# The low halves of the weights' chunks in the rwkv stage: from GpSimd to VectorE

## The chip, the cores and the metric

The kernel runs on one core of a Trainium2 chip. The metric is the time on the device in microseconds (us), the median of three runs. A core has five engines that run side by side, each through a queue of its own in a fixed order: TensorE (PE in the profile; PEld are its weight loads), VectorE (DVE), ScalarE (ACT), GpSimd (POOL) and SyncE (SP), which here only issues DMAs. An engine that waits for a semaphore holds up everything behind it in its queue.

## The reference

Two blocks of a network, one behind the other, over 512 tokens of width 1024, all in 32-bit floats. The first mixes a gated linear recurrence with dilated attention. The second takes its output and a context of 256 tokens, and has three branches: pooling, differential attention and a bidirectional rwkv recurrence, which are gated, summed and projected. A mixture of 32 experts, two per token, ends it. Cut to what matters here:

```
p_l = modulate(x, ...) @ w_in        # 1024 x 7040: pool, q, k, v, rwkv's inputs, three gates
prep_l = rwkv_prepare(rw_l, ...)     # r, k, v, decay, a, b, g from the projections
S = S * w + (S a) b + v k            # per token, 8 heads of 64 x 64, in both directions
mix = sum_n sigmoid(gate_n) * (branch_n @ w_br[n]);  x = x + mod * (mix @ w_out)
x = x + mod * hier_moe(modulate(x, ...))
```

## The kernel before

**Products in two halves.** A weight chunk (128 partitions x 1024 columns, 512 KB) is loaded by `load_chunk` (L293) on SyncE's queue into a raw buffer. `split_chunk` (L300) makes two tiles of it: the high half is a copy by ScalarE into the type float32r (L304), in which TensorE takes it; the low half is raw minus high (L305). `mm3` (L308 to 312) adds three products for each tile: high by high, high by low, low by high. Activations are split the same way by other lines. Each chunk thus has one ScalarE and one subtracting instruction; there are 125 chunks in all that are split (the w_ada and expert weights are not).

**The rwkv stage** begins at L1086. It closes the first block's weight pool and opens one with three buffers each for the high and low halves and two for the raw chunks (L1088); a raw buffer is free again when both halves are made. The recurrence is worked off in 12 batches of two chunks of 64 tokens and one direction (`batch`, L1331). `ph_a` (L1128) loads a chunk's kb and kr, makes the running sum of the decay (cs), its exponentials on ScalarE, the scaled tiles AR and BK, and the masked products AMB. `ph_i` (L1178) sends AMB through DRAM to the layout LT and inverts the triangular matrices by forward substitution on VectorE: 31 steps of a product into Tm (L1194) and a sum into Ti (L1196), each on the result of the last, 372 of each in all. The result goes through DRAM again (ttD) to `ph_b` (L1201), two batches later, which makes the states' products on TensorE and the updates on VectorE.

**Work laid between the batches.** Between and behind the batches stand projections whose chunks are split: rwkv's own inputs for the 512 tokens (`rw_prep`, 14 chunks; `rw_gate`, one), 19 of the 24 chunks of the branch gates (`gate`), the 12 half chunks of q, k and v for the differential attention, and the four of the pooling branch (`feat_tiles`, L1516). That makes 50 chunks from L1086 to L1520. Another 50 are split before, and 25 behind: five gates, 12 of `merge` (L1547), eight of the output projection (L1790). Then come the attention, the merge and the experts, whose weights (192 MB) stream in as they are used.

**What sets the order.** The order of each engine's queue is not that of the program. The Tile planner is called with schedule_with_timeline_sim: it simulates the program by its own costs and gives an engine, whenever it is free there, the next instruction that is ready there. The written order, with the numbers of gates per batch (GB, L1356), sets what is offered first. On the chip each engine then keeps to the planned order and waits where the chip is later than the plan. The DMAs of the batches (kb, kr, LT, ttD, atD) and those of the weights share SyncE's queue, so a weight load that waits for a raw buffer holds up the batch loads behind it.

Of the kernel before, what the change touches and what calls it, by code (L numbers as in the profile page):

```python
# [9 lines left out]
F32 = mybir.dt.float32  # L10
# [3 lines left out]
ALU = mybir.AluOpType  # L14
# [171 lines left out]
def build(tc, A, out, dbg=None, upto=99):  # L186
    with ExitStack() as ctx:
        _build(ctx, tc, A, out, dbg, upto)


def _build(ctx, tc, A, out, dbg, upto):
    nc = tc.nc
    V, SC, GP, PE, SY = nc.vector, nc.scalar, nc.gpsimd, nc.tensor, nc.sync
# [5 lines left out]
    cur = {}  # L199

    def weights(name, bufs, side, raw=None):

        if cur.get("wctx"):
            cur["wctx"].close()
            cur["wctx"] = None
        if bufs:
            cur["wctx"] = ctx.enter_context(ExitStack())
            cur["wp"] = cur["wctx"].enter_context(tc.tile_pool(name=name, bufs=1, side=side, reuse_waits="tile"))
            cur["wb"] = bufs
            cur["wraw"] = raw or bufs  # L210
# [3 lines left out]
    def subpool(name, nb):  # L214

        if cur.get("sub"):
            cur["sub"].close()
            cur["sub"] = None
        if nb is None:
            return  # L220
        cur["sub"] = ctx.enter_context(ExitStack())
        cur["bp"] = cur["sub"].enter_context(tc.tile_pool(name=name, bufs=1, reuse_waits="tile"))
        NB.clear()
        NB.update(nb)

    def scope(name, nb):
        subpool(None, None)
        if cur.get("ctx"):
            cur["ctx"].close()
            cur["ctx"] = None  # L230
        if nb is None:
            return
        cur["ctx"] = ctx.enter_context(ExitStack())
        cur["bp"] = cur["ctx"].enter_context(tc.tile_pool(name=name, bufs=1, reuse_waits="tile"))
        NB.clear()
        NB.update(nb)
# [5 lines left out]
    def psum(name, bufs):  # L242

        if "pctx" in cur:
            cur["pctx"].close()
        cur["pctx"] = ctx.enter_context(ExitStack())
        cur["pp"] = cur["pctx"].enter_context(tc.tile_pool(name=name, bufs=1, space=PSUM, reuse_waits="tile"))
        PB.clear()
        PB.update(bufs)
# [43 lines left out]
    def load_chunk(w, c0, kt=8, name="w", nw=128, k0=0, kn=2):  # L293

        raw = cur["wp"].tile([128, kt, nw], F32, tag="raw", name=name + "r", bufs=cur["wraw"])
        n = c0 // 128 if nw == 128 else c0 // 256 * kn + k0 // 4
        cur["ld"] = SY.dma_start(raw.rearrange("p k n -> p (k n)"), w[n]).ins
        return raw

    def split_chunk(raw, name="w"):  # L300
        kt, nw = raw.shape[1], raw.shape[2]
        hi = cur["wp"].tile([128, kt, nw], F32R, tag="hi", name=name + "h", bufs=cur["wb"])
        lo = cur["wp"].tile([128, kt, nw], F32R, tag="lo", name=name + "l", bufs=cur["wb"])
        SC.activation(hi, raw, AF.Copy)  # L304
        GP.tensor_tensor(lo, raw, hi.bitcast(F32), ALU.subtract)  # L305
        return hi, lo

    def mm3(p, ah, al, bh, bl, start, stop):  # L308
# [42 lines left out]
    def step(n=1):  # L351

        while n and fill:
            try:
                next(fill[0])
                n -= 1
            except StopIteration:
                fill.pop(0)
# [158 lines left out]
    def halves(w, c0):  # L517

        return [split_chunk(load_chunk(w, c0, kt=4, nw=256, k0=4 * kh)) for kh in range(2)]
# [12 lines left out]
    def proj_feat(w, c0, hs, n, dst, nw=256):  # L532

        for b in range(nw // 128):
            hi, lo = split_chunk(load_chunk(w, c0 + 128 * b))
            p = ps("pf")
            for k in range(8):
                mm3(p[:, :n * 128], hi[:, k, :], lo[:, k, :], hs[k][0][:, :n * 128], hs[k][1][:, :n * 128],
                    k == 0, k == 7)
            dst(b, p[:, :n * 128])  # L540
# [545 lines left out]
    weights(None, 0, None)  # L1086
    cp2 = wctx.enter_context(tc.tile_pool(name="c2", bufs=1, side="right", reuse_waits="tile"))
    weights("wp1", 3, "right", 2)  # L1088
    psum("pp2", {"mm": (2, 512), "aux": (3, 512), "ch": (1, 512), "pa": (2, 512)})
    scope("b2a", {})  # L1090
    rp = cur["bp"]
# [269 lines left out]
    def gate(n):  # L1361
        for _ in range(n):
            ngate[0] += 1
            next(gates, None)
# [152 lines left out]

    gate(24 - GL - ngate[0])
    step(99)
    subpool(None, None)  # L1520


# [24 lines left out]
    def merge(n, first=False):  # L1547

        for c in range(4):
            wh, wl_ = split_chunk(load_chunk(A["w_br"], 256 * c, kt=4, nw=256, k0=4 * n, kn=3))  # L1550
            for b in range(2):
                j = 2 * c + b
                pb = ps("pbr")
                th = mt("mth", "mth", 3)
                SY.dma_start(th, thD[:, n, j, :])
                for k in range(4):
                    mm3(pb, wh[:, k, 128 * b:128 * (b + 1)], wl_[:, k, 128 * b:128 * (b + 1)],
                        br[n][k][0], br[n][k][1], k == 0, k == 3)
                if first:
                    V.scalar_tensor_tensor(mg[j], th, 1.0, pb, op0=ALU.add, op1=ALU.mult)  # L1560
                else:
                    V.scalar_tensor_tensor(th, th, 1.0, pb, op0=ALU.add, op1=ALU.mult)
                    V.tensor_tensor(mg[j], mg[j], th, ALU.add)  # L1563
                yield
# [222 lines left out]
    for c in range(4):  # L1787
        po2 = [ps("po2", "aux" if c % 2 else "mm") for _ in range(2)]
        for kh in range(2):
            hi, lo = split_chunk(load_chunk(A["w_out_2"], 256 * c, kt=4, nw=256, k0=4 * kh))  # L1790
# [339 lines left out]
```

## Time and profile before

| | us |
|---|---|
| median of three runs | 1983.2 (1969.7 to 1985.2) |
| the profiled execution, its own time | 1981.6 |
| its span, first to last instruction | 1979.7 |
| TensorE busy (matmuls) | 1755.4, 89% |
| VectorE busy | 1091.5, 55% |
| ScalarE busy | 619.1, 31% |
| GpSimd busy | 526.5, 27% |
| granted TensorE clock, mean | 0.934 of full |

A line of the profile names the source line, the engine, the operation, the tiles it writes and reads (out<-in), their shapes, how often it ran, its busy time and the mean of one in ns, and behind a bar the idle time of its engine ahead of it, with what ended it. Busy shares are means over stages with different limits: what a change in one stage is worth is read in that stage.

### The profile page before, as it was taken

Reading aid. Unit: us, or ns where it says so; the run is one execution under the profiler, and the core shown is the slowest. Engines: PE = TensorE matmul, PEld = TensorE weight load, DVE = VectorE, ACT = ScalarE, POOL = GpSimd, SP = SyncE. Lnnn points to the kernel's source line nnn. Section 1 sums busy time; section 2 is a strip of 40 time slices with the busy share of each in tenths; the row PEclk is TensorE's granted clock in tenths of the full one; section 3 lists DMA queues with packets and bytes.
Section 4 is the critical chain, followed back from the end, with each engine's and each line's share of the span. In section 5 each row is a group of like instructions: output and inputs, shape, how many; then the busy total and the mean of one; then the engine's idle time right before and its main releaser. Section 6 shows DMA issues by size and latency. Waiting matters only on the chain. (4 is left out here: it accounts for less than half of the span.)

```text
span 1979.7 us, 31352 instructions
## 1 busy us (share of the span) xinstructions
PE 1755.4 (89%) x12309; PEld 1246.3 (63%) x12310; DVE 1091.5 (55%) x2364; ACT 619.1 (31%) x1164; POOL 526.5 (27%) x379
## 2 busy tenths in 40 slices
PE   6899998967787887888879998988979999999998
PEld 3874677953565776677667876677954545444544
DVE  4555675275487746777788655776342333332332
ACT  4234454443443222223333233443221111111110
POOL 2510337442335332231331132642310110101010
PEclk8999998988898898889898999999979999999999
DMA  8336513567546445445355338653629999999998
GB/s 298 108 111 218 197 64 103 195 181 250 156 121 171 135 137 122 109 109 137 99 151 152 81 112 280 204 179 111 246 99 387 387 386 386 386 387 386 386 386 289
DMA packets 275295, 415.89 MB, mean 210 GB/s; under 512 B 104876, under 2 KB 126408, under 8 KB 274888
## 3 DMA queue, kind: packets, MB, share of 16 engines
q1 hardware_dynamic: 246248, 383.44, 58.0%
q10 hardware_dynamic: 25568, 16.78, 2.8%
q0 software_dynamic: 3328, 13.63, 2.4%
q8 instruction: 98, 1.61, 0.3%
q14 instruction: 53, 0.43, 0.1%
HBM read 370.26 MB, written 43.53 MB: 209 GB/s over the span
## 5 line engine op out<-in xcount | busy, mean ns | idle before, releaser
L305 POOL TENSOR_TENSOR wl<-wr,wh 128x1024 fp32r<-128x1024 f32 x125 | 308.3, 2473 | 495.8 <-ACT wh L304 455.5
L304 ACT ACTIVATE wh<-wr 128x1024 fp32r<-128x1024 f32 x125 | 131.6, 1054 | 141.2 <-issue 54.9
L1980 POOL TENSOR_TENSOR yl<-ey,yh 128x512 fp32r<-128x512 f32 x30 | 38.4, 1279 | 466.1 <-ACT yh L1979 466.1
L310 PE MATMUL pf<-h2h,wh 128*128 128x512 f32 x344 | 147.8, 430 | 15.6 <-DVE Ti L1196 10.2
L1194 DVE TENSOR_TENSOR Tm<-LT,Ti 128x60 f32<-128x60 f32 (+24 forms) x372 | 116.8, 314 | 76.9 <-DMA LT<-atD 68.2
L311 PE MATMUL pf<-h2l,wh 128*128 128x512 f32 x344 | 144.5, 420 | 0.0
L312 PE MATMUL pf<-h2h,wl 128*128 128x512 f32 x344 | 143.3, 417 | 0.0
L1974 PE MATMUL ped<-wd,hid 128*64 128x512 f32 (+1 forms) x528 | 127.5, 585 | 0.7 <-ACT hid L1958 0.7
L1935 PE MATMUL peg<-wg,hTg 128*64 128x512 f32 x512 | 126.9, 597 | 0.0
L1942 PE MATMUL peu<-wu,hTg 128*64 128x512 f32 x512 | 125.3, 595 | 0.0
L1196 DVE TENSOR_TENSOR Ti<-Ti,Tm 128x60 f32<-128x60 f32 (+24 forms) x372 | 109.3, 294 | 9.1
L2007 DVE TENSOR_TENSOR acc<-acc,pcb 128x512 f32<-128x512 f32 (+1 forms) x124 | 76.0, 665 | 49.1 <-PE pcb L2006 49.0
L310 PEld LDWEIGHTS pf<-h2h,wh 128*128 128x128 f32 x344 | 69.4, 202 | 38.4 <-issue 15.4
L1974 PEld LDWEIGHTS ped<-wd,hid 128*64 128x64 f32 x528 | 39.9, 136 | 70.6 <-issue 65.9
L1942 PEld LDWEIGHTS peu<-wu,hTg 128*64 128x64 f32 x512 | 43.2, 137 | 65.1 <-issue 62.9
L311 PEld LDWEIGHTS pf<-h2l,wh 128*128 128x128 f32 x344 | 68.8, 200 | 18.5 <-issue 3.4
L1935 PEld LDWEIGHTS peg<-wg,hTg 128*64 128x64 f32 x512 | 41.9, 137 | 60.9 <-issue 58.1
L312 PEld LDWEIGHTS pf<-h2h,wl 128*128 128x128 f32 x344 | 68.6, 199 | 18.2 <-issue 2.1
L1282 PE MATMUL pW<-AMB,XV 128*128 128x64 f32 (+1 forms) x256 | 45.2, 335 | 28.7 <-DVE XV L1271 16.9
L1979 ACT ACTIVATE yh<-ey 128x512 fp32r<-128x512 f32 x30 | 18.9, 630 | 163.6 <-DVE ey L1978 90.2
L1915 DVE TENSOR_SCALAR hTg<-pg,gs,sh 128x128 f32<-128x128 f32 x64 | 25.3, 408 | 75.1 <-PE peu L1942 38.4
L1912 ACT ACTIVATE hTg<-pg,sh,gs 128x128 f32<-128x128 f32 x64 | 28.2, 457 | 121.4 <-PE peu L1942 55.4
(961 smaller groups left out, 4475.1 us busy)
## 6 DMA issues: line engine op xcount, KB each, us to landing
wg<-in_w_exp_gate_dram SPq DMA_DIRECT2D x64, 1024.0 KB
wu<-in_w_exp_up_dram SPq DMA_DIRECT2D x64, 1024.0 KB
wd<-in_w_exp_down_dram SPq DMA_DIRECT2D x62, 1024.0 KB
wr<-in_w_in_dram SPq DMA_DIRECT2D x97, 512.0 KB
kb<-kbD SPq DMA_DIRECT2D x24, 384.0 KB
wr<-in_w_out_dram SPq DMA_DIRECT2D x16, 512.0 KB
LT<-atD SPq DMA_DIRECT2D x12, 512.0 KB
thD<-mth ACTq DMA_DIRECT2D x24, 256.0 KB
```

The lines of the kernel that those rows point to most:

```text
L304: SC.activation(hi, raw, AF.Copy)
L305: GP.tensor_tensor(lo, raw, hi.bitcast(F32), ALU.subtract)
L310: PE.matmul(p, ah, bh, start=start, stop=False)
L311: PE.matmul(p, ah, bl, start=False, stop=False)
L312: PE.matmul(p, al, bh, start=False, stop=stop)
L1194: V.tensor_tensor(tmp[:, :nj, :n], bc(LT[:, s, None, ts_], [128, nj, n]), bc(T[:, js, s:s + 1], [128, nj, n]), ALU.mult)
L1196: V.tensor_tensor(T[:, js, ts_], T[:, js, ts_], tmp[:, :nj, :n], ALU.add)
L1282: PE.matmul(pw[e][:, nw * f:nw * (f + 1)], X[:, s, f, :], AMB[:, e, s, f, n0:192], start=True, stop=True)
L1935: mm = PE.matmul(pg[64 * a:64 * a + 64, :], hT[:, k, 64 * a:64 * a + 64], gp[a][k // 4][:, k % 4, :], start=(k == 0), stop=(k == 7), tile_ ...
L1942: PE.matmul(pu[64 * a:64 * a + 64, :], hT[:, k, 64 * a:64 * a + 64], up[a][k // 4][:, k % 4, :], start=(k == 0), stop=(k == 7), tile_posit ...
L1974: PE.matmul(pd[64 * a:64 * a + 64, :], hid[:, m * k + 64 * a:m * k + 64 * a + 64], dn[q][a][:, k, 0:q1 - q0], start=(k == 0), stop=(k == 3 ...
L2007: V.tensor_tensor(acc[i][:, qs], acc[i][:, qs], p, ALU.add)
```

## The change

The engine that makes the low half is looked up in the dictionary `cur` under "lo", and is GpSimd where nothing is set. It is set to VectorE (`V`) when the rwkv stage's pools are opened and taken out again behind the pooling branch. The instruction itself, its operands and its result are the same.

```diff
         SC.activation(hi, raw, AF.Copy)
-        GP.tensor_tensor(lo, raw, hi.bitcast(F32), ALU.subtract)
+        cur.get("lo", GP).tensor_tensor(lo, raw, hi.bitcast(F32), ALU.subtract)
...
     weights("wp1", 3, "right", 2)
+    cur["lo"] = V
     psum("pp2", {"mm": (2, 512), "aux": (3, 512), "ch": (1, 512), "pa": (2, 512)})
...
     gate(24 - GL - ngate[0])
     step(99)
+    cur.pop("lo")
     subpool(None, None)
```

## Rows read from the trace of the kernel before

**Rows 1.** The page: an engine's busy time, and the changed line over the span

```profile
PE 1755.4 (89%) x12309; PEld 1246.3 (63%) x12310; DVE 1091.5 (55%) x2364; ACT 619.1 (31%) x1164; POOL 526.5 (27%) x379
...
L305 POOL TENSOR_TENSOR wl<-wr,wh 128x1024 fp32r<-128x1024 f32 x125 | 308.3, 2473 | 495.8 <-ACT wh L304 455.5
```

**Rows 2.** Busy time by stretch: start:end, length, engines (instructions), clock, DMA, GB/s

```profile
480.00:1160.00 680.00, 574.47 (x5339) 465.94 (x5341) 473.16 (x1290) 225.33 (x412) 209.73 (x196) 0.89 0.50 132
1160.00:1450.00 290.00, 260.96 (x1530) 216.13 (x1526) 170.54 (x252) 111.99 (x209) 109.28 (x72) 0.96 0.56 187
1450.00:1980.00 530.00, 506.18 (x2661) 251.12 (x2661) 179.58 (x361) 71.41 (x135) 44.02 (x33) 0.98 0.97 359
```

**Rows 3.** Line 305, 480 to 1160 us: ns min/median/max; GpSimd's wait (us, times)

```profile
L305 POOL TENSOR_TENSOR wl<-wr,wh x50: 2337/2394/2582, 482.7 to 1153.2; 128x1024 fp32r<-128x1024 f32 x50
...
  ACT wh L304: 139.2, 34
```

**Rows 4.** Groups by line, 480 to 1160 us: busy us, mean ns | idle before

```profile
L312 PE MATMUL pf<-h2h,wl 128*128 128x512 f32 x286 | 120.3, 421 | 0.0
...
L304 ACT ACTIVATE wh<-wr 128x1024 fp32r<-128x1024 f32 x50 | 52.7, 1054 | 46.0 <-PE pf L311 22.4 <-issue 11.8 <-PE pt L312 6.0
...
L1194 DVE TENSOR_TENSOR Tm<-LT,Ti 128x60 f32<-128x60 f32 (+24 forms) x372 | 116.8, 314 | 76.9 <-DMA LT<-atD 68.2
L1196 DVE TENSOR_TENSOR Ti<-Ti,Tm 128x60 f32<-128x60 f32 (+24 forms) x372 | 109.3, 294 | 9.1
```

**Rows 5.** Lines 1194 and 1196, 480 to 1160 us: ns min/median/max

```profile
L1194 DVE TENSOR_TENSOR Tm<-LT,Ti x372: 152/214/5960, 535.2 to 1124.5; 128x60 f32<-128x60 f32 x18, 128x54 f32<-128x54 f32 x12, 128x66 f32<-128x66 f32 x12, 128x28 f32<-128x28 f32 x12
...
L1196 DVE TENSOR_TENSOR Ti<-Ti,Tm x372: 127/212/5912, 538.2 to 1124.7; 128x60 f32<-128x60 f32 x18, 128x54 f32<-128x54 f32 x12, 128x66 f32<-128x66 f32 x12, 128x28 f32<-128x28 f32 x12
```

**Rows 6.** Timeline of VectorE and GpSimd at five places: start us, us

```profile
488.82 2.48 POOL L305 TENSOR_TENSOR wl<-wr,wh 128x1024 fp32r<-128x1024 f32 x1
489.04 2.41 DVE L1125 COPY SI<-cst 64x256 f32<-64x256 f32 x1
...
589.13 5.96 DVE L1194 TENSOR_TENSOR Tm<-LT,Ti 128x29 f32<-128x29 f32 x1
592.70 2.34 POOL L305 TENSOR_TENSOR wl<-wr,wh 128x1024 fp32r<-128x1024 f32 x1
...
869.85 0.20 DVE L1194 TENSOR_TENSOR Tm<-LT,Ti 128x49 f32<-128x49 f32 x1
869.87 2.43 POOL L305 TENSOR_TENSOR wl<-wr,wh 128x1024 fp32r<-128x1024 f32 x1 [0.79 <-ACT wh L304]
870.08 2.28 DVE L1196 TENSOR_TENSOR Ti<-Ti,Tm 128x49 f32<-128x49 f32 x1
...
905.13 1.95 DVE L1196 TENSOR_TENSOR Ti<-Ti,Tm 128x60 f32<-128x60 f32 x1
...
1112.69 2.45 POOL L305 TENSOR_TENSOR wl<-wr,wh 128x1024 fp32r<-128x1024 f32 x1 [4.62 <-ACT wh L304]
1112.95 2.29 DVE L1194 TENSOR_TENSOR Tm<-LT,Ti 128x68 f32<-128x68 f32 x1
```

**Rows 7.** Line 1073, an add of two tiles in SBUF: ns min/median/max

```profile
L1073 DVE TENSOR_TENSOR mix<-x,mix x4: 1208/1214/1216, 407.6 to 418.6; 128x1024 f32<-128x1024 f32 x4
```

**Rows 8.** Groups by line and shape, VectorE, 550 to 1450 us

```profile
L1447 DVE TENSOR_REDUCE dss<-dsq 128x4 f32<-128x256 f32 x16 | 6.6, 412 | 2.7 <-ACT dsq L1445 2.5
L1474 DVE TENSOR_TENSOR dql<-dqT,dqh 128x512 fp32r<-128x512 f32 x8 | 5.5, 686 | 1.7 <-ACT dqh L1473 1.6
```

**Rows 9.** Waits in SyncE's queue, 480 to 1160 us: us, times, longest

```profile
SPq L297 <- POOL wl L305: 106.5, 25, 13.7
```

**Rows 10.** Waits of VectorE, 480 to 1160 us: us, times, longest

```profile
DVE Tm L1194 <- DMA LT<-atD: 68.2, 10, 11.0
DVE cs L1142 <- DMA kb<-kbD: 19.2, 8, 6.0
DVE cs L1144 <- DMA kb<-kbD: 17.4, 5, 7.0
```

## The prediction, written before the change was run

> **What bounds the kernel now.** I read the page first, then the busy time by stretch, then the one moved line, then who waits for whom. GpSimd is busy for 527 of the 1979.7 us of the span, and 308 of that is line 305 [rows 1]: it is no bottleneck by its share. The stretch table [rows 2] cuts the span at the change's borders. The 50 chunks of the rwkv stage are split between 480 and 1160 us; 75 others stay on GpSimd. In that stretch VectorE is busy 473.2 of 680 us (0.70) and TensorE 574.5. From 1450 us on the experts' weights stream at 359 GB/s on average with the DMA engines 0.97 busy; that stretch starts when what is ahead of it ends, so a shift of the rwkv stage should reach the end one for one.
>
> In the stretch the moved line is 50 instructions of 2.40 us, 120 us of GpSimd, and GpSimd stood 139.2 us waiting for the high half from ScalarE [rows 3]. TensorE does not wait for the low half: the matmuls that read it have no idle time ahead of them [rows 4]. So neither GpSimd's load nor the low half's lateness is what the change can give back.
>
> What it can give back shows on VectorE. The two lines of the triangular inverse, 1194 and 1196, have a mean of 0.314 and 0.294 us [rows 4] and a median of 0.214 and 0.212 [rows 5]: (0.100 + 0.082) us x 372 = 68 us are in a few long ones. The timeline shows when [rows 6]: the Ti of 49 elements that starts 0.21 us behind a low half of 2.43 us takes 2.28 us and ends with it, while its neighbour of the same size takes 0.20. One instruction of 5.96 us ends when a row of GpSimd instructions with a low half as its last end does. Of the 50 low halves 35 hold a VectorE instruction in this way; the first and the last of them stand there. The instructions held read SBUF alone, copies and scans among them.
>
> The Trainium skill ("SBUF — State Buffer", section "SBUF: two separate sides") says that the two engines share one pair of SBUF ports, locked for a whole instruction, and that the loser blocks fully; the trace agrees, 2.28 against 0.20 us.
>
> **The change part by part.**
> *Taken off GpSimd:* 35 holds. A full one costs VectorE 2.28 - 0.20 = 2.08 us, one that VectorE meets late 1.95 - 0.21 = 1.74 [rows 5, 6]; I take 1.9, so 66.5 us. Bounds: 59 (31 holds, without four that end longer stalls such as that of 5.96 us) and 73 (35 x 2.08).
> *Put on VectorE:* 50 instructions of 128x1024 with both inputs in SBUF. The nearest row, an add of that size, takes 1.21 us [rows 7]; the subtraction into the same output type at half the size takes 0.69 [rows 8], so 1.21 is no doubtful price. 50 x 1.21 = 60.7 us.
> The two nearly cancel: VectorE's busy time falls by about 6 of 473 us. What counts is where they lie. I treat 35 as swaps at the same place (1.9 becomes 1.21: 24.2 us less) and 15 as new work where VectorE was idle or read PSUM (18.2 us more). How much of a swap is on the path I bound by 0 and 1 and set at VectorE's busy share, 0.70: -16.9 us. Of the 15, half should fall into its idle time, which is 680 - 473 = 207 us: 18.2 x 0.5 x 0.7 = +6.4 us (bounds 0 and 18).
> *The load queue:* SyncE stood 106.5 us in 25 waits for a low half, because the next chunk's raw buffer is free only then [rows 9]. Behind it in that queue are the batches' own loads. Each low half ends 2.40 - 1.21 = 1.19 us sooner, 29.7 us in all. Those loads hold up VectorE for 68.2 + 19.2 + 17.4 = 104.8 us, 0.15 of the stretch [rows 10], so I count 0.15 x 29.7 = -4.6 us (bounds 0 and -30).
> *The new wait:* VectorE now stands at the low half until ScalarE has made the high half, and behind it in its queue are the inverses, the masks and the state updates, for which TensorE and ScalarE wait. No row shows this wait. From below it is 0; from above the 139.2 us that GpSimd stood [rows 3]. GpSimd had little else to do and was early, whereas VectorE's instructions are placed by the planner among other ready ones, so the nearer rows are two others in which VectorE reads what ScalarE has just made: 2.5 us in 16 and 1.6 us in 8 [rows 8], 0.18 us each. 50 x 0.18 x 0.7 = +6.3 us (bounds 0 and 97).
> *The pair the other way round:* GpSimd keeps 209.7 - 120 = 90 us of other work in the stretch, 0.13 of it. A low half on VectorE meets it in about 6 or 7 cases; at half a us each, and as much again for what GpSimd holds back, some +2 us. The DMAs that GpSimd issues are among that work; what waits for them lies several us ahead of its use. TensorE, ScalarE and SyncE issue the same instructions as before, and the 75 other low halves stay.
>
> Sum: -16.9 + 6.4 - 4.6 + 6.3 + 2 = -7 us. Against the profiled execution's own 1981.6 us that is 1975, 8 us below the median of 1983.2, within the 15 us by which the three runs of before differ.
>
> **The rivals.** *The low halves leave the inverses' runs.* The planner writes a new order, and VectorE's 207 idle us could take all 60.7. For it: only 0.70 of the stretch is busy, and VectorE waits for loads in blocks of up to 11 us. Against it: a low half is ready when its high half is, which is just when GpSimd hit the inverses 35 times. Each of the 35 that goes into idle time is worth another 1.21 x 0.7 = 0.85 us, so from 16 on the change is faster by 1% (19.8 us of 1983, about what a measurement of this kernel tells from no change). With all 35 it is -7 - 30 = -37 us, with the path share at 1 about -50: 1930 to 1962, say 1950.
>
> *VectorE stands for ScalarE.* The order is fixed beforehand, and a high half waits on the chip for a buffer that TensorE frees; the high halves' row has 46 us of idle time ahead of 50, half of it for TensorE [rows 4]. If VectorE inherits two fifths of GpSimd's 139.2 us, that is 56 x 0.7 = +39 instead of +6.3: 1975 + 33 = 2008. It makes the kernel slower by 1%, 2003 us, from 1.0 us a chunk on: 0.18 + (2003 - 1975) / (50 x 0.7). For it: ScalarE and TensorE themselves wait for VectorE, so the three can catch one another in turn. Against it: the 0.18 us of [rows 8].
>
> *Nothing changes* because the work only changes hands within one shared port. By the holds alone the exchange is -66.5 + 60.7 = -6 us, 1976; were the moved instruction as dear for VectorE as a hold, it would be 0, 1982: the same class as my forecast. The Trainium skill ("Perfetto Trace Analysis", section "Optimizing Scalar/DVE Operations") says that moving work between these two engines might not help because of that port; by the trace it is right about the sum of the busy times here, and silent about the new wait. That the change does not do what it says is as good as excluded: every chunk is split by the one helper.
>
> **How the numbers follow.** My own case with the unchanged case: 0.45. The low halves in idle time: 0.32, of which 0.30 goes beyond 1%. VectorE standing for ScalarE: 0.23, of which 0.20 goes beyond 1%. What is left of both lies within it. The new order alone can win or lose one of the waits for a load, up to 11 us, which is in the width of each case. So the time is 1975 us. My own case spans 1960 to 1992. The range reaches to 1938, short of the end of the faster case, and to 2010, just past the slower case's price, with about one in ten left out at either end. Faster by over 1% 0.33, within 1% 0.46, slower 0.21.
>
> **What would show it.** In the changed profile between some 480 and 1150 us: line 305 on VectorE x50 at 1.2 us; the means of lines 1194 and 1196 down to some 0.22 to 0.24 us; VectorE's busy time within 15 us of 473. My swap term is wrong if those means stay. The new-wait term is wrong if VectorE's wait for the high half is well over 15 us in all, the load-queue term if SyncE's wait for line 305 grows instead of falling by some 30 us. The forecast as a whole fails if the stage moves by more than 20 us, or if the stage ends earlier and the experts' stretch does not.

## The result: 1949.9 us, 34 us faster, and the profile after

The median went from 1984.2 us (1969.7 to 1986.2) to 1949.9 us (1948.6 to 1954.9). The ratio is 0.9852 with a 95% interval of 0.9812 to 0.9892, that is 21 to 37 us of 1984. Each group of runs has its own runs of the kernel before, whose median lay between 1978 and 1984; below, differences between kernels are therefore taken from the ratios, times 1980, which makes 29 us of this one. The profiled execution took 1948.6 us. Behind line 1089 the changed file's line numbers are one higher, from 1521 on two.

The page of the kernel after, engines first, then the three stretches of [rows 2] in the same columns:

```profile
PE 1732.8 (89%) x12309; PEld 1233.5 (63%) x12310; DVE 1062.6 (55%) x2417; ACT 618.2 (32%) x1164; POOL 406.4 (21%) x326
```

```profile
480.00:1160.00 680.00, 593.77 (x5558) 484.94 (x5560) 471.27 (x1367) 238.33 (x433) 102.24 (x149) 0.91 0.54 140
1160.00:1450.00 290.00, 241.98 (x1453) 201.13 (x1451) 160.94 (x283) 106.14 (x203) 98.15 (x59) 0.91 0.52 181
1450.00:1980.00 530.00, 483.34 (x2524) 234.16 (x2520) 162.02 (x305) 63.34 (x120) 38.39 (x30) 1.00 0.96 353
```

GpSimd lost 120 us over the span, VectorE's busy time is 29 us *lower* although it took over 53 instructions of 1.2 us. In the first stretch VectorE is as busy as before (471.3 against 473.2 us), but more work passed through it: TensorE did 5558 matmuls there instead of 5339. The last Ti ends at 1109.1 us instead of 1124.8, the first expert product starts at 1434.2 instead of 1466.9, and the span ends at 1946.8 instead of 1979.7. The 33 us won ahead of the experts reach the end one for one. TensorE was busy 22.6 us less over the span with the same 12309 matmuls (1755.4 us in [rows 1]), at a mean granted clock of 0.938 instead of 0.934, so most of the time that was won is time in which TensorE had been working. Experiment 8 takes this up.

The stage did not end at 1160 us, where [rows 2] and [rows 3] cut it: in the kernel before three more of its low halves follow, the last at 1180.9 us. In the kernel after the last one starts at 1133.0 us, 48 us sooner. Some 15 of these 48 us are lost again ahead of the experts, where the new order leaves more work: 1529 matmuls behind that point instead of 1430.

Line 305 on VectorE over the whole span (ns min/median/max), then the groups by line from 480 to 1140 us that answer to [rows 4], VectorE's waits there, and SyncE's from 480 to 1165 us:

```profile
L305 DVE TENSOR_TENSOR wl<-wr,wh x53: 1199/1220/1709, 485.5 to 1133.0; 128x1024 fp32r<-128x1024 f32 x53
```

```profile
L1195 DVE TENSOR_TENSOR Tm<-LT,Ti 128x60 f32<-128x60 f32 (+24 forms) x372 | 87.5, 235 | 43.2 <-DMA LT<-atD 35.0
L1197 DVE TENSOR_TENSOR Ti<-Ti,Tm 128x60 f32<-128x60 f32 (+24 forms) x372 | 82.4, 221 | 8.4
L305 DVE TENSOR_TENSOR wl<-wr,wh 128x1024 fp32r<-128x1024 f32 x53 | 65.1, 1228 | 32.3 <-ACT wh L304 32.0
```

```profile
DVE Tm L1195 <- DMA LT<-atD: 35.0, 5, 13.1
DVE wl L305 <- ACT wh L304: 32.0, 14, 7.7
DVE cs L1145 <- DMA kb<-kbD: 26.9, 7, 7.9
DVE cs L1143 <- DMA kb<-kbD: 23.0, 7, 8.6
```

```profile
SPq L297 <- DVE wl L305: 87.5, 22, 16.4
...
SPq L297 <- DVE Ti L1197: 36.5, 10, 14.3
...
SPq L297 <- DVE Tm L1195: 24.5, 9, 4.6
```

Four things are to be seen. The two lines of the inverse are back near their medians (0.235 and 0.221 us; 0.314 and 0.294 in [rows 4]). The low half costs VectorE 65.1 us. The new wait for the high half is 32.0 us, 0.60 us a chunk. And VectorE's wait for LT has halved, from 68.2 to 35.0 us [rows 10], which fits low halves that lie where VectorE stood, but does not show it. There are 53 of them, not 50: 22 of the 24 branch gates are split in the stage, where the description before the prediction counted 19, so 72 others stay on GpSimd and not 75.

What the holds weighed in all is worked out from the trace so: for each VectorE instruction its time beyond the shortest of its line and shape, where that is over 0.15 us and a GpSimd instruction ran beside it, from 480 to 1165 us (after: to 1140). Before it is 97.7 us, of which 83.3 lie beside a low half; after it is 22.0 us. That is 75.7 us gone.

### The profile page after: what moved, and what is told of

Its sections match the earlier page's. It is cut to its first block, busy times and chain, and to the rows that moved or that the text cites. A ratio compares the mean times of both kernels' runs of the same rounds, so it can differ in the third digit from the quotient of the medians.

```text
span 1946.8 us, 31337 instructions
## 1 busy us (share of the span) xinstructions
PE 1732.8 (89%) x12309; PEld 1233.5 (63%) x12310; DVE 1062.6 (55%) x2417; ACT 618.2 (32%) x1164; POOL 406.4 (21%) x326
## 4 chain that ended last, share of the span: by engine, by line
PE 43%; DVE 5%; DMA 5%; ACT 1%; issue 1%; SPq 0%; POOL 0%; ACTq 0%; DVEq 0%; POOLq 0%
PE ped L1976 6%; PE peg L1937 6%; PE peu L1944 6%; PE pcb L2008 3%; PE po L1799 2%; PE pg L1910 2%; DMA kb<-kbD 2%; PE pg L1911 2%; PE pW L1283 1%; PE pf L312 1%; PE pf L310 1%; PE pf L311 1%; PE pbr L310 1%; PE pbr L311 1%; PE pbr L312 1%; PE dpo L1683 1%
## 5 line engine op out<-in xcount | busy, mean ns | idle before, releaser
L305 POOL TENSOR_TENSOR wl<-wr,wh 128x1024 fp32r<-128x1024 f32 x72 | 181.3, 2528 | 306.6 <-ACT wh L304 300.2
L310 PE MATMUL pf<-h2h,wh 128*128 128x512 f32 x344 | 144.5, 420 | 20.7 <-ACT mth L1348 14.4
L1195 DVE TENSOR_TENSOR Tm<-LT,Ti 128x60 f32<-128x60 f32 (+24 forms) x372 | 87.5, 235 | 43.2 <-DMA LT<-atD 35.0
L310 PEld LDWEIGHTS pf<-h2h,wh 128*128 128x128 f32 x344 | 67.5, 196 | 40.7 <-ACT mth L1348 14.7
L1197 DVE TENSOR_TENSOR Ti<-Ti,Tm 128x60 f32<-128x60 f32 (+24 forms) x372 | 82.4, 221 | 8.4
L305 DVE TENSOR_TENSOR wl<-wr,wh 128x1024 fp32r<-128x1024 f32 x53 | 65.1, 1228 | 32.3 <-ACT wh L304 32.0
```

What stands on the lines that cost most here:

```text
L305: cur.get("lo", GP).tensor_tensor(lo, raw, hi.bitcast(F32), ALU.subtract)
L310: PE.matmul(p, ah, bh, start=start, stop=False)
L1195: V.tensor_tensor(tmp[:, :nj, :n], bc(LT[:, s, None, ts_], [128, nj, n]), bc(T[:, js, s:s + 1], [128, nj, n]), ALU.mult)
L1197: V.tensor_tensor(T[:, js, ts_], T[:, js, ts_], tmp[:, :nj, :n], ALU.add)
```

## The experiments

**Theory A:** the gain is the holds that are taken off VectorE, less a small price for the low halves, which fall into its waits, and less the new wait. **Theory B:** the planner wrote a new order of all queues (it differs on every engine), and the gain is that order's luck.

**1. Holds put back (e1_echo).** The kernel after, with GpSimd busy beside each low half:

```diff
         cur.get("lo", GP).tensor_tensor(lo, raw, hi.bitcast(F32), ALU.subtract)
+        if cur.get("lo"):
+            ec = ...                        # 128x256 bf16 scratch
+            for z in range(4):              # 256 columns of the high half each
+                GP.tensor_tensor(ec, h1, h1, ALU.subtract)
```

> The changed kernel, and behind each of the 53 high halves of the stage GpSimd subtracts the high half from itself into a small scratch tile, four instructions of 128x256 (some 0.7 us each by the AR row of before). Nobody reads the scratch; VectorE still makes the low halves. Theory A (what GpSimd's instructions held of VectorE is where the gain came from): the holds come back beside the low halves on VectorE; the means of the inverse's product and sum rise from 0.235 and 0.221 us to 0.28 or more, VectorE's time grows by 40 to 65 us and the kernel to 1985 to 2010 us. Theory B (the planner's new order alone is the gain, holds matter little): within 10 us of 1950. Theory C (the gain is SyncE's raw buffers coming free 1.2 us sooner): these do not change, so within 10 us of 1950 too.

Measured 1990.6 us, ratio 1.0026 (1.0000 to 1.0051): all of the gain is gone, as theory A expected (1985 to 2010). The groups by line, 480 to 1165 us:

```profile
L310 POOL TENSOR_TENSOR we<-wh 128x256 bf16<-128x256 f32 x202 | 165.3, 818 | 146.7 <-ACT wh L304 102.9 <-issue 33.0
...
L1202 DVE TENSOR_TENSOR Ti<-Ti,Tm 128x60 f32<-128x60 f32 (+24 forms) x372 | 106.3, 286 | 8.3
L1200 DVE TENSOR_TENSOR Tm<-LT,Ti 128x60 f32<-128x60 f32 (+24 forms) x372 | 100.6, 270 | 56.7 <-DMA LT<-atD 48.2
```

The inverse is slow again with the low halves still on VectorE. The measure of the holds is 77.0 us.

**2. and 3. Short low halves, on either engine (e2_pool_quarter, e3_dve_quarter).** Only 256 of 1024 columns are made, and the matmuls read them four times (so the low products are not the reference's):

```diff
+            lo = cur["wp"].tile([128, m, nw], F32R, ...)        # m = kt // 4
+            E.tensor_tensor(lo, raw[:, 0:m], hi[:, 0:m].bitcast(F32), ALU.subtract)   # E = GP, or V
```

> The kernel before (low halves on GpSimd), but in the stage only a quarter of each low half is made (256 of 1024 columns) and used in place of the whole, so part of the low product is left out. GpSimd's instruction falls from 2.40 to some 0.73 us and VectorE gets no new work. Theory A: 35 holds fall by 1.6 us each, 56 us of VectorE's time, and with 0.7 on the path the kernel falls to 1940 to 1950, about what the change gave or a little more. Theory B: it moves by less than 10 us from 1984, or by any amount that has nothing to do with the holds. Theory C: raw buffers come free 1.67 us sooner in 25 waits, so 1975 to 1980.

> The changed kernel (low halves on VectorE), with a quarter of each low half made and used in its place, which leaves out part of the low product. The 53 instructions fall from 1.23 to some 0.42 us, 43 us of VectorE's time. If the low halves lie on the path at VectorE's busy share of 0.7, as my forecast had it: 1915 to 1925. If they lie in VectorE's idle time, the faster rival of the forecast: 1940 to 1950, no change beyond the interval.

On GpSimd 1945.7 us, ratio 0.9806 (0.9790 to 0.9822); on VectorE 1945.2, ratio 0.9815 (0.9798 to 0.9831). With nothing put on VectorE, shortening the holds gives all of the gain. Taking 43 us of the low halves off VectorE again gives 7 us, which the two intervals do not tell from nothing. But both kernels have orders of their own, and the next group says what that can be worth.

**4. The low half without the high one (e4_no_wait).** Raw minus raw, so the low products are not the reference's, and VectorE doesn't wait for ScalarE:

```diff
-        ... .tensor_tensor(lo, raw, hi.bitcast(F32), ALU.subtract)
+        ... .tensor_tensor(lo, raw, raw if cur.get("lo") else hi.bitcast(F32), ALU.subtract)
```

> The changed kernel, but the low half in the stage is raw minus raw, so VectorE no longer reads the high half and need not wait for ScalarE; the low half's product is left out by this (it is zero). The 32 us that VectorE stood for the high half in 14 waits vanish or turn into other waits. If that wait is on the path at 0.7: some 1928. If VectorE would have stood then for something else (its loads or TensorE): 1945 to 1955, and its other waits grow by some 30 us.

Measured 1932.2 us, ratio 0.9730 (0.9703 to 0.9756): 24 us less than after, again in another order.

**5. to 7. Parts of the stage (e5_one_chunk, e6_batches_only, e7_tail_only).**

```diff
 e5:  after the first low half of the stage
+        cur.pop("lo", None)
 e6:  cur["lo"] = V from L1088, and ahead of the loop over q, k and v
+    cur.pop("lo")
 e7:  the other way round: ahead of that loop, to the end of the stage
+    cur["lo"] = V
```

> Only the first chunk of the rwkv stage has its low half made on VectorE; the other 52 stay on GpSimd. The program of before is thus changed by one instruction, but the planner writes its order anew. Theory A (the gain of some 34 us comes from the holds of VectorE that are taken away): 52 of 53 holds' causes stay, so 1980 to 1987 us, within 4 us of the kernel before. Theory B (a new order of the queues alone is worth tens of us, and the gain is the luck of one): anything; a time more than 10 us away from the kernel before in either direction speaks for it, and one below 1965 would say that a good part of the gain needs no move of the low halves at all.

> The low halves are made on VectorE only for the first 25 chunks of the stage (rwkv's own inputs, one for its gate, ten branch gates), and on GpSimd from the loop over q, k and v on. Of the time that VectorE was held beyond its normal durations in the kernel before, 43.7 us lay with the stage's first 25 low halves and 39.7 us with the later ones, some of it counted to two neighbours. Theory A (holds): the gain of 34 us splits in that proportion, so about -18 us here: 1960 to 1972 us. Theory B (order): no proportion, and this kernel and the next need not add up to -34 us. Theory C (the whole gain comes from the part without batch loads between the chunks): 1978 to 1988 us here.

> The counterpart of the run before: the low halves are made on GpSimd for the stage's first 25 chunks, and on VectorE for the 28 from the loop over q, k and v on to the pooling branch. Theory A (holds, split as 43.7 to 39.7): about -16 us: 1962 to 1974 us, and this kernel's gain and that of the one before it add up to 34 us within 8. Theory B (order): the sum is off by more than 15 us. Theory C (all of it here): 1945 to 1955 us.

| | median | ratio, 95% |
|---|---|---|
| one chunk | 2007.7 | 1.0118 (1.0088 to 1.0149) |
| first 25 | 1967.4 | 0.9925 (0.9899 to 0.9951) |
| last 28 | 1984.0 | 1.0018 (0.9990 to 1.0045) |

Only the first 25 lie where theory A put them; the other two, and the sum, are misses for it. One chunk moved costs 23 us; the two parts give -15 and +4, together -11 and not -29. In the kernel with one chunk moved the measure of the holds is 99.5 us, as before. VectorE's and SyncE's longest waits, 480 to 1165 us:

```profile
DVE Tm L1196 <- DMA LT<-atD: 75.0, 11, 12.2
```

```profile
SPq L297 <- POOL wl L305: 115.5, 22, 15.1
```

Both grew, from 68.2 and 106.5 us, but VectorE's waits for LT and kb together did not (105.9 us against 104.8), so these waits do not explain the 23 us, and where they come from stays open.

So a new order, with one low half moved, was worth 23 us here, and no difference of that size between two kernels with orders of their own (1 to 4 included) shows a cause. What stands is the grouping: the kernels with all holds in the stage took 1978 to 2008 us, those without them or with short ones 1932 to 1950. It does not hold in between: the first 25 (64.6 us of holds left) took 1967 us, but the last 28 (52.6 us left) 1984.

**8. to 10. The same in a fixed order.** The next three change a built kernel after the planning, so that the queues of all engines keep their order, instruction for instruction. The first two cut line 305's operands and point the matmuls at the quarter that is made, on the kernel before (f1_before_short) and on the kernel after (f2_after_short). The third takes the kernel of experiment 4 and gives 41 of its 53 low halves the wait for the high half (f3_wait_back).

```diff
+    for k, i in enumerate(b.instructions):           # after the planning
+        if i.name in names:                          # the 53 low halves
+            b.instructions[k] = copy.replace(i, outs=..., ins=...)      # 128x1024 -> 128x256
 f3:
+            ws.append(SyncWait(..., wait_value=...))          # ScalarE's count at the high half
+            b.instructions[k] = copy.replace(i, sync_info=SyncInfo(on_wait=ws, ...))
```

> The kernel before in its own order, which stays the same instruction for instruction on all engines: only the operands of the stage's 53 low halves are cut after the planning to 256 of 1024 columns (still on GpSimd; the matmuls read that quarter four times, so the low products are not the reference's). A GpSimd instruction of some 0.75 us holds VectorE for at most half a us where one of 2.40 held it for two. Theory A (the holds cost what the change gave back): 1942 to 1958 us, as the earlier run with short low halves on GpSimd under a new order (1945.7). Theory B (that gain, and the change's, came from a new order of the queues; one changed chunk alone had cost 26 us): 1972 to 1984 us.

> The kernel after in its own order, the same on all engines: the stage's 53 low halves on VectorE are cut after the planning to 256 of 1024 columns, 0.42 us instead of 1.23, so VectorE has 43 us less to do (the low products are not the reference's). If the low halves lie mostly in VectorE's waits, as the earlier run of this size under a new order said: 1941 to 1948 us. By the share of the path that the prediction used, 0.7: 1950 - 30 = 1920 us.

> The kernel of the run in which VectorE's low half does not read the high half (1932.2 us), in its own order, with the wait for the high half put back, after the planning, at the 41 of 53 chunks where the high half stands first in that order (the low half is still raw minus raw, so not the reference's). Theory A (the wait itself is what the change lost): 18 x 41 / 53 = 14 us slower than without it, 1942 to 1952 us. Theory B (the 18 us between that run and the change came from the other order): 1930 to 1936 us.

| | median | ratio, 95% |
|---|---|---|
| f1, before, short | 1937.5 | 0.9779 (0.9750 to 0.9808) |
| f2, after, short | 1937.3 | 0.9778 (0.9753 to 0.9803) |
| f3, wait put back | 1940.8 | 0.9793 (0.9766 to 0.9821) |

f1 settles it: 44 us (38 to 50; 40.5 by the medians of its group) by shortening GpSimd's 53 instructions in the order of before. All three runs lie 1 to 5 us below the range that theory A, or idle time in f2, gave them, and outside the others' ranges. f1's groups by line, 480 to 1165 us, and a place in its timeline (start us, us):

```profile
L1196 DVE TENSOR_TENSOR Ti<-Ti,Tm 128x60 f32<-128x60 f32 (+24 forms) x372 | 89.8, 242 | 9.1
L1194 DVE TENSOR_TENSOR Tm<-LT,Ti 128x60 f32<-128x60 f32 (+24 forms) x372 | 89.5, 241 | 91.3 <-DMA LT<-atD 82.7
...
L305 POOL TENSOR_TENSOR wl<-wr,wh 128x256 fp32r<-128x256 f32 (+1 forms) x55 | 44.8, 814 | 232.6 <-ACT wh L304 191.3 <-DMA TT<-ttD 29.9 <-PE pi L1260 11.2
```

```profile
858.38 0.18 DVE L1194 TENSOR_TENSOR Tm<-LT,Ti 128x30 f32<-128x30 f32 x1
858.52 0.72 POOL L305 TENSOR_TENSOR wl<-wr,wh 128x256 fp32r<-128x256 f32 x1 [0.21 <-ACT wh L304]
858.60 0.69 DVE L1196 TENSOR_TENSOR Ti<-Ti,Tm 128x30 f32<-128x30 f32 x1
...
859.55 0.18 DVE L1194 TENSOR_TENSOR Tm<-LT,Ti 128x29 f32<-128x29 f32 x1
```

The stage from 480 us to the start of its last low half, before and in f1, in the columns of [rows 2]:

```profile
480.00:1180.90 700.90, 595.37 (x5473) 482.86 (x5474) 483.27 (x1306) 234.04 (x426) 214.64 (x200) 0.89 0.49 131
480.00:1140.70 660.70, 568.51 (x5473) 463.06 (x5474) 421.54 (x1306) 233.66 (x426) 130.43 (x200) 0.92 0.54 139
```

For the same 1306 instructions VectorE is busy 61.7 us less, and the stage is 40.2 us shorter. The measure of the holds falls from 97.7 to 39.4 us, and the time by 44: a us of hold is worth 0.75 us (0.65 to 0.85 by the interval). VectorE's wait for LT got *longer* (82.7 against 68.2 us [rows 10]): some of what the holds cost comes back as waiting.

TensorE's two numbers show how the rest reaches the end. Of the 40.2 us only 13.3 are idle time of TensorE (105.5 us before, 92.2 in f1); 26.9 are its busy time, for the same 5473 matmuls at a granted clock of 0.92 of the full 2.4 GHz instead of 0.89. The lower level of that clock, 1.2 GHz, was granted for 154 us of the stage before and for 106 in f1, and 628 matmuls fell into it before, 355 in f1. In the kernel before it fell, for example, at 584 us, where TensorE had just stood 2.3 us for ScalarE; the next matmul of line 311 took 0.63 us instead of 0.39. So the 0.75 holds both: TensorE waits less, and it spends less time at the lower level. No run here parts the two.

Two rivals remain in f1, and the waits speak against both. The raw buffers come free sooner: over the same loads SyncE's wait for line 305 fell from 128.0 us (480 to 1190 us, before) to 94.4 (480 to 1150 us, f1). But VectorE's waits for LT and kb, whose loads stand behind them in SyncE's queue, grew from 104.8 to 122.2 us, and ScalarE's high halves waited 5.9 us for raw chunks where they had waited 5.0. And GpSimd's other results come sooner: in the whole stage before, TensorE, VectorE and ScalarE waited 5.6 us for GpSimd, so by the waits that is the most it could give.

f2 measures the price of the low halves on VectorE: 65.1 - 22.8 = 42.3 us less work for 0.0074 x 1980 = 14.7 us, 0.35 us each. The intervals of the two ratios leave 5 to 24 us for this difference, so 0.13 to 0.57 each. Its row, and its waits, 480 to 1165 us:

```profile
L305 DVE TENSOR_TENSOR wl<-wr,wh 128x256 fp32r<-128x256 f32 x53 | 22.8, 430 | 38.4 <-ACT wh L304 38.2
```

```profile
DVE Tm L1195 <- DMA LT<-atD: 38.8, 5, 14.6
DVE wl L305 <- ACT wh L304: 38.2, 17, 9.8
```

Where the low halves lie shows in the timeline of the kernel after (VectorE's only, start us, us):

```profile
848.22 1.23 DVE L305 TENSOR_TENSOR wl<-wr,wh 128x1024 fp32r<-128x1024 f32 x1
849.36 0.20 DVE L1195 TENSOR_TENSOR Tm<-LT,Ti 128x49 f32<-128x49 f32 x1
849.98 1.23 DVE L305 TENSOR_TENSOR wl<-wr,wh 128x1024 fp32r<-128x1024 f32 x1 [0.41 <-ACT wh L304]
851.12 0.69 DVE L1157 TENSOR_TENSOR BK<-kb,em 128x512 f32<-128x512 f32 x1
851.72 0.20 DVE L1197 TENSOR_TENSOR Ti<-Ti,Tm 128x49 f32<-128x49 f32 x1
```

Here two of them do stand between steps of an inverse, and one makes VectorE wait 0.41 us. It is the sum over 53 that is cheap, not each.

f3 measures the wait: 41.4 us of it cost (0.9793 - 0.9730) x 1980 = 12.5 us, 0.30 us each (5 to 20 us, 0.12 to 0.48, by the intervals); by the medians 8.6. Not all of this wait is new standing: VectorE stood 51.4 us in all ahead of the low halves in f3, and 30.4 in experiment 4, there for the raw chunk and for TensorE. VectorE's wait in f3, 480 to 1165 us:

```profile
DVE wl L305 <- ACT wh L304: 41.4, 18, 8.3
```

**The account.** Holds: -75.7 x 0.75 = -57. Low halves on VectorE: 65.1 x 0.35 = +23. Wait: 32.0 x 0.30 = +10. Together -24 us, against a measured -29 (-21 to -37). The intervals of the three shares make the sum uncertain by some 17 us either way, an estimate that takes them as independent. The 5 us that are left for the order lie within that: the weight of the holds is shown, the size of the order's part in this change is not.

**11. and 12. Further versions (e8_all, e9_hi_too).**

```diff
 e8, against the kernel before:
-        GP.tensor_tensor(lo, raw, hi.bitcast(F32), ALU.subtract)
+        V.tensor_tensor(lo, raw, hi.bitcast(F32), ALU.subtract)
 e9, against the kernel after: low halves as in e8, and in the rwkv stage
-        SC.activation(hi, raw, AF.Copy)
+        V.tensor_copy(hi, raw)
```

> All 125 low halves of the program are made on VectorE, so also the 50 ahead of the rwkv stage and the 22 or so behind it. In the kernel before, the low halves of the first 480 us held VectorE for 66 us beyond its normal durations and those between 1160 and 1450 us for 21 us. Theory A (holds count, and the low half itself lies mostly in VectorE's idle time): a further gain where VectorE is on the path; if the share is that of the rwkv stage (34 of 83 us, 0.4), 0.4 x 87 = 35 us more, so 1905 to 1945 us. Rival (ahead of 480 us the projections are bound by TensorE and the loads, not by VectorE, so holds there cost nothing, and the wait of VectorE for the high half delays its evictions): no further gain or a loss, 1945 to 1975 us.

> All 125 low halves on VectorE, and in the rwkv stage the high halves there too, as a copy of about 1.2 us ahead of the subtraction, so VectorE waits for no other engine between raw chunk and low half. Against the run with all low halves on VectorE (1923.0 us): theory A (VectorE's idle time takes such work at a small price, and the wait for ScalarE cost up to 18 us): 1903 to 1923 us. Rival (with 64 us more VectorE is the bound of the stage, and the high half that ScalarE made in 1.05 us beside it now comes late): 1930 to 1965 us.

1923.0 us, ratio 0.9707 (0.9675 to 0.9739), and 1915.6 us, ratio 0.9679 (0.9662 to 0.9695). Both beat the changed kernel, by 1.5 and 1.8%; their intervals overlap, so which of them is better is open. Of e8's gain over the kernel after 18.5 us come ahead of the stage (the last h2l ends at 452.6 us instead of 471.1), where the measure of the holds falls from 60.0 to 5.4 us; the rest comes behind. In e9 the high half on VectorE took 0.74 us, not the 1.2 expected (groups by line, 480 to 1165 us):

```profile
L305 DVE CAST wh<-wr 128x1024 fp32r<-128x1024 f32 x49 | 36.1, 736 | 14.8 <-DMA wr<-in_w_in_dram 9.7 <-PE pf L314 4.3 <-PE pt L315 0.5
```

## Why the prediction was right and where it was wrong

The time lay in the range, and on the rival "the low halves leave the inverses' runs" (0.32, 1930 to 1962, say 1950) rather than on my own case of -7 us. That it met that case's 1950 to the us is luck: the case priced 35 low halves at nothing and took the rest of the sum as in mine, whereas the runs give -57, +23 and +10 us. By the test named last, a stage that moves by more than 20 us, my own forecast failed: the experts start 32.7 us sooner.

- **What bounds.** Right. VectorE's holds were what could be given back; f1 shows it in a fixed order, and e1 and e2 agree.
- **Price of the instruction.** Right: 1.21 us forecast, 1.220 measured; 60.7 us forecast for 50, 65.1 measured for 53. The three that were missed lie behind 1160 us.
- **The swap, the step that failed.** I gave a hold and the low half that replaces it the same share of the path, 0.70, and so kept only their difference, 24.2 us. For the holds the share was right (0.75 in f1). For the low halves it is 0.35 in f2 (at most 0.57). The reading, argued and not shown chunk by chunk: a hold strikes while VectorE is in a run of dependent steps, whereas a low half is placed by the planner and can stand where VectorE waits for LT, kb or TensorE. The holds were also more than my 66.5 us: 75.7 us went. Five holds of 2.8 to 6.0 us, where a low half ends a row of GpSimd instructions as in [rows 6], carry 21.9 of the 83.3 us that lay beside low halves; at 1.9 each they were counted as 9.5. The two terms measured are -57 and +23 where the forecast had -16.9 + 6.4.
- **TensorE's clock** (no term). The sum had nothing for it; TensorE issues the same instructions. Its busy time fell all the same, by 22.6 us over the span here, where 850 matmuls ahead of the experts fell into the lower level instead of 967, and by 26.9 us in the stage in f1. The share of 0.70 came near the 0.75 without this part, which is luck.
- **The load queue** (-4.6). Not borne out: over the same loads SyncE's wait for the low half fell from 128.0 to 87.5 us, but waits of 61.0 us behind Ti and Tm came up that the kernel before did not have, so 148.5 in all. VectorE's own waits for those loads fell all the same, from 104.8 to 84.9 us, which no run here divides between causes.
- **The new wait** (+6.3). Its sign was right, its size too small: 32.0 us against the 9 us that 0.18 us a chunk gave, past the 15 us named as the test. Its share of the path was smaller than taken (0.30), so it cost 10. The rival that lived on this wait needed 1.0 us a chunk; it was 0.60.
- **The pair the other way** (+2). The low halves' side is small, as said: 53 x (1.228 - 1.199) = 1.5 us over the shortest. But the holds of VectorE beside GpSimd's other work grew from 14.4 to 22.0 us, which the 75.7 already counts.
- **The new order.** I allowed it the 11 us of one lost wait. One chunk alone (e5) moved the time by 23, so that allowance was too small, and a single timing of the change could have come out near zero with the same mechanism.

The Trainium skill ("Perfetto Trace Analysis", section "Optimizing Scalar/DVE Operations") says that a move between these two engines might not help because of their shared port. By the two sums it nearly held: 75.7 us of holds left VectorE and 65.1 us of low halves came. By the path it did not: the kernel is 1.5% faster.

## What to carry to other kernels

Price work that is added to an engine and stalls that are taken off it with separate shares: here a us of stall counted 0.75 and a us of work that the planner could place 0.35, and why the second is smaller is argued and not shown. If GpSimd works on large SBUF tiles beside a chain of short VectorE instructions, look for a mean far above the median on VectorE, and see in the timeline whether the long ones end with a GpSimd instruction. Compare TensorE's busy time for the same number of matmuls as well as its waits: two thirds of what f1 won in the stage showed there. Where a planner rewrites the order, time an edit of little weight first, or change operands in a fixed order; in this kernel one moved chunk was worth 1.2%, so a difference of that size between two orders shows no cause.

## What the runs showed of the hardware

A hold does not always end with the GpSimd instruction that it began beside. In the kernel after, a Ti of 30 elements begins beside two DMA issues of GpSimd and ends with the multiply behind them (start us, us):

```profile
602.63 1.77 POOL L777 DMA_DIRECT2D kbD<-nb  x2 [1.98 <-DVE Tm L1195]
...
603.54 3.34 DVE L1197 TENSOR_TENSOR Ti<-Ti,Tm 128x30 f32<-128x30 f32 x1
...
604.37 2.46 POOL L825 TENSOR_TENSOR tha<-tha,kt 128x1024 f32<-128x1024 f32 x1
```

It ran until 606.88 us and the multiply until 606.83: 3.34 us for an instruction whose neighbours take 0.19. On VectorE the plain copy of a 128x1024 tile into float32r took 0.74 us (e9), the subtraction into the same type 1.23 us (the kernel after).
